# A hybrid encoder layer on one core: the second half's scaled rows are made ahead and kept in DRAM, and TensorE's part of interleaved steps gets a later place in the scheduler's order

## The chip, the cores and the metric

The kernel runs on one NeuronCore of a Trainium2 chip. The metric is the device time of one execution in microseconds (us); before the change it is 1823.78 us, the median of three runs (1821.98 to 1827.82). TensorE (PE in the profile; PEld are its weight loads) multiplies, VectorE (DVE) and ScalarE (ACT) work elementwise, GpSimd (POOL) takes small elementwise work, and SyncE (SP) issues nearly all DMAs from one queue, in order.

## The reference

One encoder layer is applied to two groups of tokens, 1024 (sample) and 256 (prompt), 1280 rows of 2048 features in all, with shared weights. Each group also has 256 memory tokens.

```python
def layer(x, mem, norm_g, w_in, ...):
    hn = rms_norm(x, norm_g)
    proj = hn @ w_in                                   # 2048 -> 4896 columns
    xbc, z_ssd, dt_raw, q, k, v, z_att, mq, z_mem = split_cols(proj, IN_SIZES)
    xbc = silu(centred_dwconv(xbc, conv_w, conv_b))    # 5 taps
    ...                                                # two SSD scans, forward and backward
    o_ssd = rms_norm(y * silu(z_ssd), ssd_norm_g)
    o_att = window_attention(rms_norm(q), rms_norm(k), v, sink) * silu(z_att)
    memn = rms_norm(mem, mem_norm_g)
    mk, mv = split_cols(memn @ w_mem_kv, ...)
    o_mem = softmax(rms_norm(mq) @ rms_norm(mk).T) @ mv * silu(z_mem)
    return x + concat([o_ssd, o_att, o_mem]) @ w_out
```

All inputs are float32.

## The kernel before

**Products in three matmuls.** Every float32 factor of the big products is split into a high part (rounded to the matmul's type, `wh`, `xH`) and a low part (`wl`, `xL`, the rest); a product is high x high + low x high + high x low. A weight tile is loaded into `wraw` (SP, `RB` = 4 buffers), ScalarE writes the high part and VectorE the low part (`wsplit`, lines 200 to 206; `WB` = 3 buffers each). So a *weight block* is one load, one or two pairs of splits, and 12 to 21 matmuls.

**Stages.** The 1280 rows are taken in two halves of 640 (grp 0: sample rows 0 to 639; grp 1: the rest). In order: the products with the memory weights (`mk`, `mv`, 32 blocks of 12 matmuls 128x512), the `q` block of half 0 (16 blocks of 15), the *pair stage* of half 0 (`pairs_in(0)`: 10 units of 8 blocks of 21 matmuls 128x320), the `kv` block (16 of 15, 288 wide) and the `mq` block (16 of 15) of half 0, the pair stage of half 1, and then blocks with *lane steps* beside them, and last the output product.

The pair stage is one level of a Strassen-like scheme with seven products per block (`block_pair`, `seven`): its weights need sums made by GpSimd (`weight_sums`, tile `ws`, split into `sh` and `sl`), and its rows need sums of rows (`p_sums`, split by `p_split` into `tH`, `tL`). At the end of each unit the seven results are added together (`ev_seven`, whose helper tile `yu` has the tag `xst`), and conv or gate work on them is queued in `left`.

**Rows.** Before a half can be multiplied, its rows must be scaled by the norm's gain and by 1/rms of each token (`rbc`, made by `x_rows` with ten small matmuls from `rx`). `rx` needs the sum of squares of each token: `stats` loads pieces of 128x512 and ScalarE squares them with a running sum. `x_stats` does that for half 0; `stage_stats` (before) does it for the remaining five x tiles (20 pieces) and the four tiles of memory tokens (16 pieces), tile `sst`, one buffer with the tag `xst`, called from `pairs_in(0)` at five of the eight blocks of a unit.

For half 1, `t_step` then runs beside the `kv` and `mq` blocks. It loads row tiles from the input (`p_load`), scales them and stores the scaled tile in DRAM (`p_scale`, `xs_d`), makes the sums and splits them, and from step 23 on loads the stored tiles again (`r_load`) and fills `xH`, `xL` of half 1 (`r_fill`, `p_rows`).

**Lanes.** Attention, SSD and memory attention for tiles of 128 tokens are generators in two queues (`lanes`). `pump` takes steps from them after each weight block at fixed rates; `step` runs a generator up to its next `yield`. A step's instructions go to all engines, TensorE's among them, as small matmuls and transposes between those of the weight blocks.

**Order.** The program is not run in the order in which it is written. Every instruction gets a running number; a scheduler fills each engine's queue with what is ready by its own estimate, the lowest number first. `tc.high_priority(offset=n)` gives a lower number by n; a negative offset gives a later one. `tc.issue_after(marks)` queues an instruction behind the last weight split on its own engine. Weight splits and evictions have offsets of 30 to 100 (`HP`). The queues so made are fixed: on the chip each engine works in that order and waits where an operand isn't there.

Of the kernel before, what the change touches and what calls it, by code (L numbers as in the profile page):

```python
# [10 lines left out]
F32 = mybir.dt.float32  # L11
F32R = mybir.dt.float32r
# [13 lines left out]
HP = (30, 100, 100)  # L26
MR = ((1.75, 0), (1.75, 0))
# [14 lines left out]
def hymba_encoder_kernel(  # L42
# [7 lines left out]
    V, A, G, T, S = nc.vector, nc.scalar, nc.gpsimd, nc.tensor, nc.sync  # L50
# [215 lines left out]
    def block_feat(name, evac):  # L266

        ps = [[acc.tile([P, 512], F32, tag="acc", name="acc") for _ in range(2)] for _ in range(2)]
        src = laid_in(name)
        hls = {}  # L270
        for kk in range(KT // 2):
            raw = wp.tile([P, 512], F32, tag="wraw", name="wraw", bufs=RB)
            S.dma_start(raw, src[kk])
            with tc.high_priority(offset=HP[2]):
                h = wp.tile([P, 2, 256], F32R, tag="wh", name="wh", bufs=WB)
                l = wp.tile([P, 2, 256], F32R, tag="wl", name="wl", bufs=WB)
                wsplit(raw, h.rearrange("p a c -> p (a c)"), l.rearrange("p a c -> p (a c)"))
            hls[kk] = h, l
            if kk == KT // 2 - 2:
                continue  # L280
            tail = kk == KT // 2 - 1

            for kks in ([(kk - 1, kk)] if tail else [(kk,)]):
                for f in range(2):
                    for k in [2 * x + j for x in kks for j in range(2)]:
                        q, m = divmod(k, 4)
                        sh, sl = [x[:, k % 2, f * P:(f + 1) * P] for x in hls[k // 2]]
                        for half in range(2):
                            c = slice(half * 320, half * 320 + 320)
                            o = ps[f][half][:, :320]  # L290
                            T.matmul(o, sh, cur["H", q][:, m, c], start=(k == 0), stop=False)
                            T.matmul(o, sh, cur["L", q][:, m, c], start=False, stop=False)
                            T.matmul(o, sl, cur["H", q][:, m, c], start=False, stop=(k == KT - 1))
                    if tail and f == 0:
                        with tc.high_priority(offset=HP[1]):
                            evac(0, ps[0])
            for k in range(2 * kks[0], 2 * kk + 2):
                yield k
        with tc.high_priority(offset=HP[1]):
            evac(1, ps[1])  # L300


    def ev_gate(c, base):
        def f(i, ps):
            z = ev.tile([P, 512], F32, tag="evt" if i % 2 else "evu", name="zs")
            A.activation(z, ps, AF.Tanh, scale=0.5)
            V.scalar_tensor_tensor(out=z, in0=z, scalar=1.0, in1=ps, op0=ALU.add, op1=ALU.mult)
            S.dma_start(z_d[c][base + i], z)
        return f

    def ev_gateT(c, grp, f0):
        def f(fc, ps):
            z = ev.tile([P, 640], F32, tag="evu", name="zs")
            for b in range(2):
                zb, p = z[:, b * 320:b * 320 + 320], ps[b][:, :320]
                A.activation(zb, p, AF.Tanh, scale=0.5)
                V.scalar_tensor_tensor(out=zb, in0=zb, scalar=1.0, in1=p, op0=ALU.add, op1=ALU.mult)
            S.dma_start(zT_d[c][grp][:, f0 + fc, :], z)
        return f
# [24 lines left out]
    def conv_work(grp, fc, u):  # L344
# [5 lines left out]
        def first_tap():  # L350
            c.append(ev.tile([P, 650], F32, tag="evt", name="c")[:, :n])
            A.activation(c[0], u[:, :n], AF.Identity, scale=cw[0], bias=vec[:, R_CB + fc:R_CB + fc + 1])
# [26 lines left out]

    def ev_conv(grp, f0):  # L380
        us = []

        def f(fc, ps):
            fc = f0 + fc
            u = ev.tile([P, 650], F32, tag="evu", name="u")
            V.tensor_copy(u[:, 0:4], carry[:, fc, :])
            V.memset(u[:, 388:392], 0.0)
            V.memset(u[:, 648:650], 0.0)
            A.activation(u[:, 4:324], ps[0][:, :320], AF.Copy)
            A.activation(u[:, 324:388], ps[1][:, :64], AF.Copy)  # L390
            A.activation(u[:, 392:648], ps[1][:, 64:320], AF.Copy)
            us.append(u)
            if len(us) == 2:
                left.extend(conv_two(*[conv_work(grp, f0 + i, us[i]) for i in range(2)]))
        return f
# [85 lines left out]
    def k_prep(t):  # L481
# [3 lines left out]
        ss = sm.tile([P, 2], F32, tag="s2", name="kss", bufs=4)  # L485
# [3 lines left out]
        rr = sm.tile([P, 2], F32, tag="s2", name="krr", bufs=4)  # L489
# [109 lines left out]
    def attn(t):  # L599
# [13 lines left out]
        ss = sm.tile([P, 8], F32, tag="s8", name="qss", bufs=4)  # L613
        V.reduce_sum(out=ss, in_=hv(sq), axis=AX.X)
        r = sm.tile([P, 8], F32, tag="s8", name="qr", bufs=4)
# [27 lines left out]
        def scores(rr):  # L643
            lg = mp.tile([P, 2, 385], F32, tag="lg", name="lg", bufs=2)
            G.tensor_copy(lg[:, :, nk:nk + 1], ns8[:, rr, :].unsqueeze(2))  # L645
            nm = sm.tile([P, 2], F32, tag="m2", name="nm", bufs=10)
# [8 lines left out]
            den = sm.tile([P, 2], F32, tag="m2", name="den", bufs=10)  # L655
# [57 lines left out]
    def mem_attn(t):  # L713
# [26 lines left out]
        def scores(hp):  # L740
# [8 lines left out]
            m = sm.tile([P, 2], F32, tag="m2", name="mm", bufs=10)  # L749
# [3 lines left out]
            den = sm.tile([P, 2], F32, tag="m2", name="mden", bufs=10)  # L753
# [53 lines left out]
    def ssd_up(t):  # L807
# [27 lines left out]
        cbd = sm.tile([P, 2], F32, tag="s2", name="cbd", bufs=4)  # L835
        V.reduce_sum(out=cbd, in_=cd2, axis=AX.X)
        dco = sm.tile([P, 16], F32, tag="dco", name="dco", bufs=2)
# [166 lines left out]
    def ssd_down(t):  # L1004
# [3 lines left out]
        ss = sm.tile([P, 2], F32, tag="s2", name="yss", bufs=4)  # L1008
# [39 lines left out]
        rs = sm.tile([P, 2], F32, tag="s2", name="yrs", bufs=4)  # L1048
# [177 lines left out]
    def p_load(k, grp=0):  # L1226

        raw[k] = [rp.tile([P, 640], F32, tag="ch", name=n, bufs=CH) for n in ("ra", "rb_")]
        for i in range(2):
            r = k + 8 * i  # L1230
            S.dma_start(raw[k][i], x_turned[grp, r * P:(r + 1) * P, :])

    def p_scale(k, grp=0):

        for i, x in enumerate(raw[k]):
            r = k + 8 * i
            V.scalar_tensor_tensor(out=x, in0=x, scalar=vec[:, R_G + r:R_G + r + 1], in1=rbc, op0=ALU.mult, op1=ALU.mult)
            if grp:
                S.dma_start(xs_d[r], x)

    def p_rows(k, tiles):

        for i, x in enumerate(tiles):
            q, j = divmod(k + 8 * i, 4)
            if j == 0:
                new_quad(q)
            h, l = cur["H", q][:, j, :], cur["L", q][:, j, :]
            A.activation(h, x, AF.Copy)
            V.tensor_sub(l, x, h.bitcast(F32))

    def p_fill(k):
        p_scale(k)
        p_rows(k, raw[k])
# [9 lines left out]
    def r_fill(k):  # L1263
        p_rows(k, again.pop(k))
# [14 lines left out]

    p_plan = {}  # L1280
    for k in range(8):
        at = (9, 12, 15, 17, 20, 22, 25, 27)[k]
        sums_at = (at + 1, 32, 34)[max(0, k - 5)]
        for j, f in ((at - 2, p_load), (at, p_fill), (sums_at, p_sums), (sums_at + 1, p_split)):
            p_plan.setdefault(j, []).append((f, k))

    def p_step(j):
        if j == 9:
            need(x_rows, [0])
        with ExitStack() as st:  # L1290
# [4 lines left out]
            for f, k in sorted(p_plan.get(j, ()), key=lambda x: ((p_split, p_sums, p_fill, p_load).index(x[0]), x[1])):  # L1295
# [11 lines left out]
    def t_step(j):  # L1307
        with ExitStack() as st:
# [4 lines left out]
            for f, k in t_plan.get(j, ())[::-1]:  # L1313
                f(k)

    def ev_seven(kind, f0, grp):
# [3 lines left out]
        def begin(u):  # L1320
# [9 lines left out]
            else:  # L1330
                tiles = [ev.tile([P, 650], F32, tag="evu", name="r") for _ in range(2)]
# [210 lines left out]
    squares = stage_stats()  # L1542
# [4 lines left out]
    def pairs_in(grp, extra):  # L1547
# [16 lines left out]
    pairs_in(0, p_step)  # L1564
    for _ in squares:
        pass
    for _ in x_rows(1):
        pass
# [11 lines left out]
    pairs_in(1, t_step)  # L1580
# [183 lines left out]
```

## Time and profile before

| | |
|---|---|
| median of three runs | 1823.78 us (1821.98 to 1827.82) |
| profiled execution, its own time | 1824.83 us |
| its span, first to last instruction | 1823.1 us |
| granted TensorE clock, mean | 0.995 |
| TensorE busy | 1778.3 us, 98% |
| VectorE, ScalarE, GpSimd busy | 1328.4, 950.1, 673.6 us |
| DMA traffic | 329 MB, mean 180 GB/s |

How to read the lines: a group line has the source line, the engine, the operation, out<-in by tile names and the shape, then the count, busy time, mean duration in ns, and the idle time of the engine just before. In the view of waits a row says which engine and tile waited for what: us in total, number of times, longest. In the view of windows each row is a stretch of time with the busy us and number of instructions of each engine, the granted clock, the share of DMA in use and GB/s. In the view of the time line a row is start, duration, engine, line, operation and in brackets the idle time before it and what ended it. A matmul's end is modelled, so short gaps between matmuls don't show as idle time.

### The profile page before, as it was taken

Reading aid. Unit: us, or ns where it says so; the run is one execution under the profiler, and the core shown is the slowest. Engines: PE = TensorE matmul, PEld = TensorE weight load, DVE = VectorE, ACT = ScalarE, POOL = GpSimd, SP = SyncE. Lnnn points to the kernel's source line nnn. Section 1 sums busy time; section 2 is a strip of 40 time slices with the busy share of each in tenths; the row PEclk is TensorE's granted clock in tenths of the full one; section 3 lists DMA queues with packets and bytes.
Section 4 is the critical chain, followed back from the end, with each engine's and each line's share of the span. In section 5 each row is a group of like instructions: output and inputs, shape, how many; then the busy total and the mean of one; then the engine's idle time right before and its main releaser. Section 6 shows DMA issues by size and latency. Waiting matters only on the chain.

```text
span 1823.1 us, 30989 instructions
## 1 busy us (share of the span) xinstructions
PE 1778.3 (98%) x10306; PEld 1572.7 (86%) x10306; DVE 1328.4 (73%) x2473; ACT 950.1 (52%) x2081; POOL 673.6 (37%) x1092
## 2 busy tenths in 40 slices
PE   9999999999999999999999999999999999999999
PEld 7788999999799999987777877887777787889998
DVE  5595678888878889787667767767787765766665
ACT  6554545553454444366567447666547644543332
POOL 0115778870168889411001110001111101048774
PEclk9999999999999999999999999999999999999999
DMA  8685544446853343374545577656688765654442
GB/s 296 196 315 192 152 142 146 128 146 206 265 189 91 114 117 110 106 219 133 162 136 155 165 241 267 207 173 213 220 282 259 238 212 161 201 154 147 142 139 81
DMA packets 213873, 328.96 MB, mean 180 GB/s; under 512 B 21904, under 2 KB 84688, under 8 KB 213712
## 3 DMA queue, kind: packets, MB, share of 16 engines
q1 hardware_dynamic: 213568, 326.92, 57.8%
q8 instruction: 81, 1.33, 0.3%
q14 instruction: 80, 0.66, 0.1%
q10 hardware_dynamic: 144, 0.06, 0.0%
HBM read 250.29 MB, written 76.61 MB: 179 GB/s over the span
## 4 chain that ended last, share of the span: by engine, by line
PE 65%; DMA 12%; issue 8%; DVE 6%; POOL 5%; ACT 3%; SPq 1%; ACTq 0%; POOLq 0%; DVEq 0%
PE acc L257 8%; PE acc L256 8%; PE acc L258 8%; PE acc L1207 7%; PE acc L1205 7%; PE acc L1206 7%; POOL ws L1177 3%; PE accm L1206 3%; PE accm L1205 3%; PE accm L1207 3%; PE py L937 2%; DVE wl L204 1%; DMA wraw<-in_w_in_pairs_dram 1%; DMA rf<-ac 1%; POOL wraw L1177 1%
## 5 line engine op out<-in xcount | busy, mean ns | idle before, releaser
L257 PE MATMUL acc<-wl,xH 128*128 128x512 f32 (+1 forms) x1248 | 479.0, 384 | 8.0 <-DVE wl L204 7.7
L256 PE MATMUL acc<-wh,xH 128*128 128x512 f32 (+1 forms) x1248 | 484.3, 388 | 1.6 <-ACT wh L203 1.5
L258 PE MATMUL acc<-wh,xL 128*128 128x512 f32 (+1 forms) x1248 | 476.0, 382 | 0.0
L204 DVE TENSOR_TENSOR wl<-wraw,wh 128x512 fp32r<-128x512 f32 (+1 forms) x480 | 351.8, 736 | 145.7 <-ACT wh L203 140.5
L203 ACT ACTIVATE wh<-wraw 128x512 fp32r<-128x512 f32 (+1 forms) x480 | 290.8, 612 | 211.1 <-PE acc L258 126.7
L257 PEld LDWEIGHTS acc<-wl,xH 128*128 128x128 f32 x1248 | 236.1, 189 | 54.9 <-DVE wl L204 13.6
L256 PEld LDWEIGHTS acc<-wh,xH 128*128 128x128 f32 x1248 | 236.1, 189 | 45.7 <-ACT wh L203 3.6
L258 PEld LDWEIGHTS acc<-wh,xL 128*128 128x128 f32 x1248 | 235.7, 189 | 42.1 <-issue 0.7
L1177 POOL TENSOR_TENSOR ws<-wraw 128x128 f32<-128x128 f32 x224 | 144.8, 646 | 340.9 <-DMA wraw<-in_w_in_pairs_dram 210.2
L203 ACT ACTIVATE sh<-ws 128x384 fp32r<-128x384 f32 x224 | 115.7, 523 | 272.9 <-PE acc L1206 131.2
L204 DVE TENSOR_TENSOR sl<-ws,sh 128x384 fp32r<-128x384 f32 x224 | 156.2, 700 | 136.9 <-ACT sh L203 132.5
L1177 POOL TENSOR_TENSOR ws<-wraw,ws 128x128 f32<-128x128 f32 x224 | 149.1, 666 | 17.3
L1177 POOL TENSOR_TENSOR ws<-ws,wraw 128x128 f32<-128x128 f32 x224 | 152.8, 682 | 0.0
L1177 POOL TENSOR_TENSOR wraw<-wraw 128x128 f32<-128x128 f32 x224 | 138.9, 620 | 17.5
L645 POOL COPY lg<-nsink 128x2 f32<-128x2 f32 x40 | 17.3, 433 | 268.9 <-PE ppt L673 138.9
L1205 PE MATMUL acc<-xH,wh 128*128 128x320 f32 x320 | 99.5, 311 | 3.7 <-ACT wh L203 3.7
L1207 PE MATMUL acc<-xH,wl 128*128 128x320 f32 x320 | 99.2, 310 | 3.3 <-DVE wl L204 3.3
L1205 PE MATMUL acc<-tH,sh 128*128 128x320 f32 x320 | 99.1, 310 | 1.0 <-ACT qs L324 1.0
L1207 PE MATMUL acc<-tH,sl 128*128 128x320 f32 x320 | 99.2, 310 | 0.0
L1206 PE MATMUL accm<-tL,wh 128*128 128x320 f32 x320 | 99.1, 310 | 0.0
L1205 PE MATMUL accm<-tH,wh 128*128 128x320 f32 x320 | 99.0, 310 | 0.0
L1206 PE MATMUL acc<-xL,wh 128*128 128x320 f32 x320 | 99.0, 309 | 0.0
(479 smaller groups left out, 3921.1 us busy)
## 6 DMA issues: line engine op xcount, KB each, us to landing
wraw<-in_w_in_pairs_dram SPq DMA_DIRECT2D x160, 256.0 KB, 2.8
wraw<-in_w_in_laid_dram SPq DMA_DIRECT2D x128, 256.0 KB, 3.7
wraw<-in_w_out_laid_dram SPq DMA_DIRECT2D x64, 256.0 KB, 3.3
wraw<-in_w_out_pairs_dram SPq DMA_DIRECT2D x64, 256.0 KB, 2.9
xH<-xH SPq DMA_DIRECT2D x16, 640.0 KB, 5.9
xL<-xL SPq DMA_DIRECT2D x16, 640.0 KB, 6.5
rf<-ac SPq DMA_DIRECT2D x40, 256.0 KB, 4.0
rb<-ac SPq DMA_DIRECT2D x40, 256.0 KB, 4.4
```

What stands on the lines that cost most here:

```text
L203: a = A.activation(h, raw, AF.Copy)
L204: b = V.tensor_sub(l, raw, h.bitcast(F32))
L256: T.matmul(ps[t][:, :n], sh, h[:, :n], start=(k_ == 0), stop=False)
L257: T.matmul(ps[t][:, :n], sh, l[:, :n], start=False, stop=False)
L258: T.matmul(ps[t][:, :n], sl, h[:, :n], start=False, stop=(k_ == last))
L645: G.tensor_copy(lg[:, :, nk:nk + 1], ns8[:, rr, :].unsqueeze(2))
L937: T.matmul(py[:, h * 64:h * 64 + 64], mt[:, (h % 4) * P:(h % 4 + 1) * P], xsT[g][:, h * 64:h * 64 + 64], start=True, stop=True)
L1177: G.tensor_tensor(out=o, in0=x, in1=y, op=op)
L1205: T.matmul(ps[p], h, xh, start=(k_ == 0), stop=False)
L1206: T.matmul(ps[p], h, xl, start=False, stop=False)
L1207: T.matmul(ps[p], l, xh, start=False, stop=(k_ == 7))
```

## The change

It has two parts, and some tidying.

First, the scaled rows of half 1 are made during the pair stage of half 0. The generator `first_side` takes the place of `stage_stats` there: it squares the 20 pieces of the five remaining x tiles, runs `x_rows(1)`, and then for each of the 16 row tiles loads it, scales it on VectorE and stores it in `xs_d`. `t_step` loads the scaled tiles (`p_next`) and no longer scales; its steps and those of the second filling move by a few places, and the second filling writes into the row tiles that are there (`new=False`) instead of taking new ones. The 16 pieces of the memory tokens are squared by `next_side`, called in the pair stage of half 1. Both generators use one buffer of their own, tag `sq`.

Second, TensorE's operations go through an object `Later`: those issued inside a lane step, except steps of `x_stats` and `x_rows`, get a number later by `LATE` = 20.

Beside that, unused functions are removed, small tiles move from the pool `sm` to `mp`, and some tiles are cut to the width that they use.

```diff
+LATE = 20
...
-    V, A, G, T, S = nc.vector, nc.scalar, nc.gpsimd, nc.tensor, nc.sync
+    V, A, G, S = nc.vector, nc.scalar, nc.gpsimd, nc.sync
+
+    class Later:
+        inside = False
+
+        def __getattr__(self, op):
+            def issue(*args, **kw):
+                with tc.high_priority(offset=-LATE) if self.inside else ExitStack():
+                    return getattr(nc.tensor, op)(*args, **kw)
+            return issue
+
+    T = Later()
...
                 for ins in marks:
                     st.enter_context(tc.issue_after(ins))
+                T.inside = name[0] not in ("x_stats", "x_rows")
+                st.callback(setattr, T, "inside", False)
                 next(gen)
...
-        ss = sm.tile([P, 2], F32, tag="s2", name="kss", bufs=4)
+        ss = mp.tile([P, 2], F32, tag="s2", name="kss", bufs=4)
...
-    def p_scale(k, grp=0):
-
-        for i, x in enumerate(raw[k]):
-            r = k + 8 * i
-            V.scalar_tensor_tensor(out=x, in0=x, scalar=vec[:, R_G + r:R_G + r + 1], in1=rbc, op0=ALU.mult, op1=ALU.mult)
-            if grp:
-                S.dma_start(xs_d[r], x)
+    def x_row(grp, r):
+        return x_turned[grp, r * P:(r + 1) * P, :]
+
+    def scale_row(r, x):
+        V.scalar_tensor_tensor(out=x, in0=x, scalar=vec[:, R_G + r:R_G + r + 1], in1=rbc, op0=ALU.mult, op1=ALU.mult)
...
-            if j == 0:
+            if new and j == 0:
                 new_quad(q)
...
-        p_rows(k, again.pop(k))
+        p_rows(k, again.pop(k), new=False)
...
+    def p_first(k):
+        p_load(k, lambda r: x_row(0, r))
+
+    def p_next(k):
+        p_load(k, lambda r: xs_d[r])
...
-        at = (3, 6, 9, 12, 15, 17, 19, 21)[k]
-        for j, f in ((at - 2, lambda k: p_load(k, 1)), (at, lambda k: p_scale(k, 1)), (at + 1, p_sums), (at + 2, p_split)):
+        at = (4, 7, 10, 13, 15, 17, 19, 21)[k]
+        for j, f in ((at - 3, p_next), (at, p_sums), (at + 2, p_split)):
             t_plan.setdefault(j, []).append((f, k))
-    for k, at in enumerate((25, 27, 29, 31, 32, 33, 35, 37)):
+    for k, at in enumerate((25, 26, 27, 28, 29, 31, 33, 35)):
         for j, f in ((at - 2, r_load), (at, r_fill)):
...
-    def stage_stats():
-
-        yield from stats([(xrow(t), t) for t in range(5, 10)] + [(mrow(i), 10 + i) for i in range(4)],
-                         lambda i: fin.tile([P, 512], F32, tag="xst", name="sst"), ahead=1, group=3)
+    def square_place(_):
+        return fin.tile([P, 640], F32, tag="sq", name="sst")[:, :512]
+
+    def first_side():
+
+        yield from stats([(xrow(t), t) for t in range(5, 10)], square_place, ahead=1)
+        for _ in x_rows(1):
+            yield
+        for r in range(KT):
+            x = fin.tile([P, 640], F32, tag="sq", name="xrow")
+            S.dma_start(x, x_row(1, r))
+            yield
+            with ExitStack() as st:
+                for ins in marks:
+                    st.enter_context(tc.issue_after(ins))
+                scale_row(r, x)
+                S.dma_start(xs_d[r], x)
+            yield
+
+    def next_side():
+        yield from stats([(mrow(i), 10 + i) for i in range(4)], square_place, ahead=1)
...
-                if k in (0, 2, 4, 5, 7):
-                    next(squares, None)
+                if grp == 0 and (u > 3 or k not in (3, 7)) or grp and k in (0, 2, 4):
+                    next(side, None)
...
-    pairs_in(0, p_step)
-    for _ in squares:
-        pass
-    for _ in x_rows(1):
-        pass
+    side = first_side()
+    pairs_in(0, p_step, side)
+    assert next(side, None) is None
...
-    pairs_in(1, t_step)
+    side = next_side()
+    pairs_in(1, t_step, side)
+    assert next(side, None) is None
```

More of the change, by code (lines that the diff above doesn't have):

```diff
@@ L264, in block_tok @@
             yield k
[L266 to L300, printed above, removed]
     def ev_gate(c, base):
@@ L1007, in ssd_down @@
         tok = slice(t * P, (t + 1) * P)
-        ss = sm.tile([P, 2], F32, tag="s2", name="yss", bufs=4)
+        ss = mp.tile([P, 2], F32, tag="s2", name="yss", bufs=4)
         if not last:
@@ L1047, in ssd_down @@
                 yield
-        rs = sm.tile([P, 2], F32, tag="s2", name="yrs", bufs=4)
+        rs = mp.tile([P, 2], F32, tag="s2", name="yrs", bufs=4)
         rsqrt(rs, ss, 1.0 / 512, 2)
@@ L1330, in begin @@
             else:
-                tiles = [ev.tile([P, 650], F32, tag="evu", name="r") for _ in range(2)]
+                tiles = [ev.tile([P, 640], F32, tag="evu", name="r") for _ in range(2)]
             r0, r1 = [hv(x[:, o:o + 640], 2) for x in tiles]
@@ L1541, in hymba_encoder_kernel, with pairs_in @@
     units = [(i // 2, i % 2 * 2) if i < 4 else (None, 2 * (i - 4)) for i in UNITS]
-    squares = stage_stats()
     owe = 0.0
     keep = [(q, i, j) for q in range(4) for i in range(2) for j in (0, 2)]
-    def pairs_in(grp, extra):
+    def pairs_in(grp, extra, side):
         nonlocal owe
```

60 lines of the change are left out of this document (18 added, 42 removed).

## The prediction

> **What bounds the kernel now.** I read the page's first part, then the windows cut where the kernel's stages change, then TensorE's waits in the stages that lose time, then the rows of the tiles behind those waits.
>
> ```profile
> span 1823.1 us, 30989 instructions
> PE 1778.3 (98%) x10306; PEld 1572.7 (86%) x10306; DVE 1328.4 (73%) x2473; ACT 950.1 (52%) x2081; POOL 673.6 (37%) x1092
> ```
> ```profile
> core 0: us, PE busy (x) PEld busy (x) DVE busy (x) ACT busy (x) POOL busy (x), PEclk, DMA share, GB/s
> 0.00:152.00 152.00, 148.07 (x636) 120.21 (x637) 96.55 (x160) 82.32 (x151) 18.11 (x37) 1.00 0.81 273
> 152.00:413.00 261.00, 252.59 (x1688) 248.44 (x1687) 194.03 (x300) 132.04 (x272) 201.39 (x318) 0.99 0.48 142
> 413.00:445.00 32.00, 30.58 (x233) 30.35 (x232) 25.62 (x47) 11.59 (x23) 3.03 (x4) 1.00 0.60 189
> 445.00:505.00 60.00, 55.61 (x242) 43.79 (x241) 51.78 (x80) 27.36 (x47) 9.29 (x12) 0.98 0.83 267
> 505.00:750.00 245.00, 245.00 (x1652) 243.54 (x1651) 203.93 (x324) 117.24 (x207) 203.93 (x304) 0.99 0.40 120
> 750.00:1560.00 810.00, 787.62 (x4252) 638.71 (x4251) 584.62 (x1293) 477.82 (x1207) 88.40 (x162) 1.00 0.64 199
> ```
> TensorE is the bound: 98% busy, and the change neither adds nor removes a matmul. Only its idle time is at stake. By stage (window minus PE busy): memory projections and the q block 152 - 148.07 = 3.9 us; the first half's pair blocks 261 - 252.59 = 8.4; the kv block 1.4; the mq block 4.4; the second half's pair blocks 0; the blocks with lane steps 810 - 787.62 = 22.4.
>
> The two pair stages do the same matmuls, and the second loses nothing. What differs is the side work, and these rows show how it hurts:
>
> ```profile
> PE acc L1205 <- ACT wh L203: 3.7, 5, 1.2
> PE acc L1207 <- DVE wl L204: 3.3, 7, 0.8
> ```
> ```profile
> L1392 ACT ACTIVATE sst<-sst x36: 613/632/637, 154.7 to 401.3; 128x512 f32<-128x512 f32 x36
> L1392 ACT ACTIVATION_READ_ACCUMULATOR sst<-sst x36: 182/187/189, 155.3 to 401.8; 128x1 f32 x36
> ...
>   ACT sst L1392: 52.4, 29
> ...
> DMA to landing us min/median/max: 2.8/3.3/5.8
> ```
> ```profile
> SPq L1401 <- DVE u L1351: 22.1, 5, 5.8
> SPq L1401 <- ACT sst L1392: 35.4, 23, 3.2
> ```
> ```profile
> 314.99 0.62 ACT L1392 ACTIVATE sst<-sst 128x512 f32<-128x512 f32 x1
> ...
> 319.65 0.63 ACT L1392 ACTIVATE sst<-sst 128x512 f32<-128x512 f32 x1 [0.29 <-DMA sst<-in_mem_sample_dram]
> ...
> 323.71 0.64 ACT L1392 ACTIVATE sst<-sst 128x512 f32<-128x512 f32 x1 [2.11 <-DMA sst<-in_mem_sample_dram]
> ...
> 328.43 0.63 ACT L1392 ACTIVATE sst<-sst 128x512 f32<-128x512 f32 x1 [3.06 <-DMA sst<-in_mem_sample_dram]
> ```
> The 36 squares of the first half's pair stage share one buffer (tag xst), also with the evictions' yu. So each load waits for the square before it (and, at a unit's end, up to 5.8 us for an eviction), each square for its load: a chain of 3.3 landing + 0.63 + 0.19 = 4.1 us, and the three distances above, 4.66, 4.06 and 4.72, agree; I take 4.2. ScalarE does its work in order, so the splits wh and sh behind a waiting square are late, and after a group of four TensorE stops at the next unit: 3.7 + 3.3 = 7.0 us.
>
> **What goes.** (a) The changed kernel gives the squares a buffer of their own (tag sq). In its built order no square stands between the 9th and the 76th of the 80 weight blocks of that stage. So the 7.0 us at unit starts go, and with them a stretch at half clock that followed one of them:
>
> ```profile
> 253.20:256.60 3.40, 3.40 (x15) 0.50 0.51 152
> 502.40:509.20 6.80, 6.08 (x14) 0.50 0.95 327
> ```
> At full clock the second pair stage starts a matmul every 245 / 1652 = 0.148 us, so 3.4 us would hold 23, not 15: 8 x 0.148 = 1.2 us. Together -8.2.
>
> The Trainium skill (TensorE: Matmul & The Clock Gate, section HAM oscillation) warns of gaps over some 3.4 us. This trace is stricter: the single idle times before both stretches are all under 1.5 us, and the clock was halved nevertheless.
>
> (b) The second half's 16 scalings and 16 stores leave the row filling in the kv and mq blocks:
>
> ```profile
> PE acc L257 <- DVE wl L204: 4.2, 6, 1.4
> PE acc L256 <- ACT wh L203: 1.5, 2, 1.1
> ```
> ```profile
> L1237 DVE SCALAR_TENSOR_TENSOR ra<-ra,vec,rbc x16: 876/879/1082, 76.7 to 481.8; 128x640 f32<-128x640 f32 x16
> ```
> TensorE loses 4.2 + 1.5 = 5.7 us there. The half-clock stretch costs more: 14 matmuls in 6.8 us, where at the 0.237 us of the first window (148.07 us, with 624 block matmuls and a dozen small ones) 29 fit: 15 x 0.237 = 3.6 us. VectorE sheds 16 x 0.88 = 14 us. But the worst cluster, just before 502, stands at the second filling of the x rows, which stays and is even put on consecutive steps (25 to 29). I count half of 9.3 us: -4.6, bounds 0 and -9.3.
>
> (c) Lane matmuls get a number 20 later. What they lose now:
>
> ```profile
> PE pst L867 <- DVE fl L888: 3.1, 2, 2.0
> ...
> PE psc L651 <- ACT qT L635: 0.3, 1, 0.3
> ```
> These are the first and last of 15 kinds of lane wait that, with one of a weight split, make up the 22.4 us of the last window. Their cause is the scheduler's guess: a lane matmul is put where its operand should be ready, and the operand comes 0.3 to 2 us later. A later number helps only where priority, not readiness, set the place. In the built order lane matmuls do move back, by 5 to 8 of the 15 matmuls of a weight block in the mean. But their feeding operations move back too: of 500 lane matmuls that wait for something, those with under 2 us of matmuls between the last matmul that their operand depends on and themselves fall from 135 to 100, while the median distance doesn't change and some get shorter (probability transposes pmt among them). A quarter fewer tight places would be 0.26 x 22.4 = -6; new tight ones could give +4. I take -2.
>
> **What comes.** Durations of the two kinds of chain:
>
> ```profile
> xst<-in_x_sample_dram SPq DMA_DIRECT2D x20, 256.0 KB, 4.3
> ...
> ra<-in_x_turned_dram SPq DMA_DIRECT2D x16, 320.0 KB, 3.8
> zT<-th SPq DMA_DIRECT2D x16, 320.0 KB, 2.8
> ```
> ```profile
> L204 DVE TENSOR_TENSOR wl<-wraw,wh 128x512 fp32r<-128x512 f32 (+1 forms) x480 | 351.8, 736 | 145.7 <-ACT wh L203 140.5
> L203 ACT ACTIVATE wh<-wraw 128x512 fp32r<-128x512 f32 (+1 forms) x480 | 290.8, 612 | 211.1 <-PE acc L258 126.7
> ```
> The cover is the splits' lead: three buffers, so a split may run while two blocks of matmuls remain, in the pair stage 2 x 21 x 0.148 = 6.2 us less 0.61 + 0.74 and the sums' splits, some 4 us.
>
> (d) Eight of the 20 squares of the other x rows are pulled ahead into the memory projections' end: in the built order the first stands after weight block 23 and the eighth after block 33. One buffer, and DMAs at a share of 0.81: 4.3 + 0.63 + 0.19 = 5.1 us each, so 7 x 5.1 = 35.7 us, against nine blocks of 12 and one of 15 matmuls, 123 x 0.237 = 29.2. The surplus is 6.5. There the lead is nearly used up by the 20 squares before them, so I take +5 (0 to +6.5). The other 12 stand 5 us apart in the q block and the first units, further than their chain.
>
> (e) The 16 squares of the memory tokens, planned for the second pair stage, are pulled before it: nothing holds their ScalarE part back, and the scheduler sees ScalarE free. In the built order 14 stand between weight block 76 of the first pair stage and block 15 of the kv block: 13 x 4.2 = 54.6 us, against 4 x 21 x 0.148 + 15 x 2.0 (32 us for 16 kv blocks) = 42.4. Surplus 12.2, less the lead of 4 to 6: +7 (0 to +12). SP's weight loads queue behind these loads too, each held until the square before it is done.
>
> (f) The 16 rows scaled ahead share that one buffer: store, then load, then scaling, 2.8 to 3.6 + 3.8 + 0.88, some 7.8 us with the nearest rows, 7.6 with the lighter traffic here. VectorE waits for the load, and the splits wl and sl stand behind it; SP waits for the store with weight loads behind it. The built order spreads the 16 scalings over 34 blocks, 34 x 3.11 = 105.7 us; 15 x 7.6 = 114. Surplus 8, less the lead: +4 (0 to +9). VectorE's 14 us of extra work themselves are free: the second pair stage runs it at 203.93 / 245 = 83% without loss, and here it would be at (194 + 14) / 261 = 80%.
>
> By the Trainium skill (DMA: Bandwidth & Descriptors, section on the anatomy of one DMA: 2.0 us fixed and the bytes at 436 GB/s) a 320 KB transfer would take an estimated 2.75 us, a row 6.4 us, and (f) would be nothing; the rows above, 2.8 and 3.8, don't agree for loads.
>
> (g) Stalls of several us in (d) and (e) bring half-clock stretches: 1.2 us for one as in (a), 3.6 for a double one: +3.
>
> The tile renames, the moved small tiles, the removed unused functions and 16 more loads (5 MB, at a DMA share near 0.5) cost nothing.
>
> Sum: -8.2 - 4.6 - 2 + 5 + 7 + 4 + 3 = +4.2. The profiled execution took 1824.83 us, so 1829.0. That is 1 us above the median of 1823.78, a difference I don't correct for.
>
> **The rivals.** *Faster: the chains are hidden.* The lead recovers between squares, and chains at their shortest landing of 2.8 leave only +3 of (d) to (g); then -8.2 - 4.6 - 6 + 3 = -16: 1809; with (b) at its best -9.3, 1804; with the lanes at -2, 1813. For it: squares with a buffer of their own start their load earlier than now. Against it: 29 of the 36 sst squares waited for their load. Chance 0.28, decided by landing plus square staying within some 3.7 us: 13 x 3.7 = 48 leaves (e) inside the lead. The price of the Trainium skill's page above lies on this side, for the rows alone.
>
> *Slower: the square chain owns the kv block.* The row chain (f) has eaten the lead just before the first memory-token square comes; then the surpluses aren't covered: 6.5 + 12.2 + 8 + 3 against 8.2 + 4.6 + 2: +15, 1840. It decides from a lead under 1 us at block 75. For it: rows and squares follow each other in the same buffer. Chance 0.32.
>
> *Nothing gained in lanes and the filling, (b) and (c) zero or worse:* +11, 1836; its chance is in the one before.
>
> *The change does not do what it says:* the later number moves no matmul. The built order excludes it.
>
> **How the numbers follow.** This kernel can be told from no change at about 0.3%, 5.5 us. My forecast, the partial trade of stalls, has 0.40; its own range is 1822 to 1836, so of it 0.27 lies within 0.3% and 0.13 slower. The faster case gives 0.27 faster and 0.01 same, the slower one 0.28 slower and 0.04 same. So faster 0.27, same 0.32, slower 0.41. Range 1811 to 1842: it reaches from the hidden chains to the bare ones.
>
> **What would show it.** Right: no idle time of TensorE at unit starts before 260 us; sst squares around 400 to 440 us 4 us apart, each with a DMA wait; kv blocks longer than 2.0 us; VectorE waiting for DMA xrow; lane waits near 20 us. Wrong: the window of the kv block still loses under 2 us (then e fails), VectorE's waits for xrow under 5 us in all (f fails), or lane waits under 12 us (c was underrated).

## The result, and the profile after

The changed kernel takes 1841.64 us (median of four runs, 1840.2 to 1844.44), the kernel before beside it 1823.5: a ratio of 1.0097, with a 95% interval of 1.0077 to 1.0118. It is slower by 18 us. (One run of the kernel before, of 2147 us at a granted clock of 0.753, is left out of all comparisons.) The forecast was 1829.0; the result lies at the upper edge of the range (1811 to 1842) and 1.6 us from the rival "slower: the square chain owns the kv block" (1840).

The first part of the page after the change:

```profile
span 1842.7 us, 31031 instructions
PE 1795.1 (97%) x10306; PEld 1579.8 (86%) x10306; DVE 1329.8 (72%) x2473; ACT 951.6 (52%) x2081; POOL 671.4 (36%) x1092
```

TensorE's matmuls are the same in number, but it is busy 16.8 us longer and idle 2.8 us longer. More busy time for the same matmuls means here that the clock was halved for a time or that matmuls followed each other at a slower pace; both are seen below. To see where, both profiles are cut where each stage issues its first block matmul. The columns are those of the windows in the prediction. First the kernel before:

```profile
0.00:154.00 154.00, 150.07 (x644) 121.89 (x645) 96.55 (x160) 82.42 (x151) 19.71 (x40) 1.00 0.81 274
154.00:414.40 260.40, 251.99 (x1691) 248.16 (x1690) 195.43 (x303) 132.81 (x272) 199.79 (x314) 0.99 0.48 140
414.40:447.80 33.40, 31.98 (x244) 31.75 (x242) 27.02 (x49) 13.05 (x26) 3.03 (x4) 1.00 0.62 192
447.80:512.00 64.20, 59.81 (x243) 46.54 (x242) 50.67 (x77) 27.80 (x47) 13.43 (x20) 0.95 0.84 275
512.00:757.50 245.50, 245.50 (x1682) 245.49 (x1681) 206.51 (x332) 115.77 (x205) 199.78 (x296) 1.00 0.38 114
757.50:1621.40 863.90, 841.51 (x4470) 681.70 (x4469) 623.06 (x1354) 503.15 (x1249) 97.84 (x178) 1.00 0.64 198
```

The changed kernel, at the same six stages:

```profile
0.00:166.70 166.70, 156.88 (x645) 124.25 (x645) 97.54 (x163) 90.83 (x182) 21.68 (x46) 0.97 0.81 267
166.70:426.60 259.90, 252.53 (x1691) 248.75 (x1690) 210.56 (x311) 117.65 (x219) 203.32 (x302) 0.99 0.51 160
426.60:469.10 42.50, 36.88 (x243) 35.07 (x242) 28.66 (x57) 21.71 (x50) 3.87 (x8) 0.92 0.68 206
469.10:525.40 56.30, 55.00 (x243) 44.95 (x241) 41.28 (x70) 29.93 (x51) 14.22 (x22) 1.00 0.80 255
525.40:772.20 246.80, 246.22 (x1682) 245.95 (x1681) 199.99 (x320) 112.77 (x199) 195.39 (x296) 1.00 0.36 108
772.20:1641.90 869.70, 850.42 (x4470) 683.91 (x4470) 622.09 (x1354) 503.51 (x1249) 92.79 (x178) 0.99 0.64 197
```

Half clock comes in stretches of 3.4 us or 6.8 us in these two profiles. Such a stretch is counted here with half its length: a stage's length times (1 - granted clock). "At full clock" below means that this is taken off.

| stage | before | after | difference | of it half clock |
|---|---|---|---|---|
| memory projections and q block | 154.0 | 166.7 | +12.7 | +5.1 |
| first pair stage | 260.4 | 259.9 | -0.5 | 0 |
| kv block | 33.4 | 42.5 | +9.1 | +3.4 |
| mq block | 64.2 | 56.3 | -7.9 | -3.4 |
| second pair stage | 245.5 | 246.8 | +1.3 | 0 |
| blocks with lane steps | 863.9 | 869.7 | +5.8 | +3.4 |
| output product | 201.7 | 200.8 | -0.9 | 0 |

The sum is +19.6, the difference of the spans. (The profiled execution after, 1844.44 us, is the longest of the four, so it is more than the 18 us of the medians.) In the kv block the time line of ScalarE shows the forecast chain of squares (start, duration, and in brackets the idle time before and what ended it):

```profile
426.52 0.63 ACT L1346 ACTIVATE sst<-sst 128x512 f32<-128x512 f32 x1 [2.78 <-DMA sst<-in_mem_sample_dram]
...
430.63 0.63 ACT L1346 ACTIVATE sst<-sst 128x512 f32<-128x512 f32 x1 [3.39 <-DMA sst<-in_mem_sample_dram]
...
431.26 1.09 ACT L217 ACTIVATE wh<-wraw 128x288 fp32r<-128x288 f32 x3
434.90 0.63 ACT L1346 ACTIVATE sst<-sst 128x512 f32<-128x512 f32 x1 [2.56 <-DMA sst<-in_mem_sample_dram]
```

The squares start 4.1 and 4.3 us apart, each after waiting for its load, and the weight splits are done in a bunch between them. TensorE's waits in this stage:

```profile
PE acc L59 <- ACT wh L217: 4.2, 2, 3.0
PE acc L59 <- DVE wl L218: 1.0, 2, 0.6
```

In the changed kernel all of TensorE's operations carry line 59, the line of `Later`; the tile names tell them apart.

### The profile page after: what moved, and what is told of

Same layout as the page of the kernel before. It is cut to its first block, busy times and chain, and to the rows that moved or that the text cites. A ratio compares the mean times of both kernels' runs of the same rounds, so it can differ in the third digit from the quotient of the medians.

```text
span 1842.7 us, 31031 instructions
## 1 busy us (share of the span) xinstructions
PE 1795.1 (97%) x10306; PEld 1579.8 (86%) x10306; DVE 1329.8 (72%) x2473; ACT 951.6 (52%) x2081; POOL 671.4 (36%) x1092
## 5 line engine op out<-in xcount | busy, mean ns | idle before, releaser
L59 PE MATMUL acc<-wh,xH 128*128 128x512 f32 (+1 forms) x1248 | 490.8, 394 | 10.3 <-ACT wh L217 8.6
L59 PE MATMUL acc<-wl,xH 128*128 128x512 f32 (+1 forms) x1248 | 489.7, 392 | 8.9 <-DVE wl L218 8.2
L59 PE MATMUL acc<-wh,xL 128*128 128x512 f32 (+1 forms) x1248 | 487.9, 391 | 0.0
L59 PEld LDWEIGHTS acc<-wh,xH 128*128 128x128 f32 x1248 | 237.9, 191 | 59.6 <-ACT wh L217 11.9
L1127 POOL TENSOR_TENSOR ws<-wraw 128x128 f32<-128x128 f32 x224 | 146.5, 654 | 259.4 <-DMA wraw<-in_w_in_pairs_dram 93.0
L1127 POOL TENSOR_TENSOR ws<-wraw,ws 128x128 f32<-128x128 f32 x224 | 153.8, 687 | 17.6
L1127 POOL TENSOR_TENSOR ws<-ws,wraw 128x128 f32<-128x128 f32 x224 | 148.4, 663 | 0.0
L595 POOL COPY lg<-nsink 128x2 f32<-128x2 f32 x40 | 12.5, 314 | 285.7 <-PE ppt L59 118.5
L59 PE MATMUL acc<-tL,sh 128*128 128x320 f32 x320 | 98.7, 308 | 0.0
```

Source lines behind the costliest of these rows:

```text
L59: return getattr(nc.tensor, op)(*args, **kw)
L1127: G.tensor_tensor(out=o, in0=x, in1=y, op=op)
```

## The experiments

**The later number alone, and the rows alone.** The first kernel is the one before with `Later` and `LATE = 20`; the second is the changed one without them:

```diff
-    T = Later()
+    T = nc.tensor
...
-                T.inside = name[0] not in ("x_stats", "x_rows")
-                st.callback(setattr, T, "inside", False)
```

> The kernel before with one part of the change: lane matmuls numbered 20 later; rows and squares as before. In its built order TensorE passes from weight blocks to lane matmuls 465 times (222 before, 466 in the changed kernel). Theory S (the later number costs by itself: the alternation adds small losses at each passage, more than the distances won give back): the stages up to 757 us stay as before, the lane stage takes 869 to 872 us instead of 863.9, the time is 1829 to 1833 us. Rival R (readiness, step (c) of the prediction: the shift is neutral or gains, and the lane stage's +5.8 us in the changed kernel came from the moved small tiles, the cut buffers or another starting point): lane stage 858 to 865, time 1817 to 1825.

> The changed kernel without the later number: the rows scaled ahead, the squares' own buffer and all tidying stay. Theory S with the stage sums of the two traces (+2.9 +9.7 -0.5 +9.0 -7.9 +1.3 -0.9, and 0 in the lane stage): 1835 to 1838 us, lane stage 864 +- 2, kv stage 42, memory and q stages 12 us over before. Rival R: the lane stage keeps its +5.8 and the time is that of the changed kernel, 1841.

Measured: the later number alone 1828.3 us, ratio 1.002 (1.0004 to 1.0036), so some 3.7 us, between the ranges of theory S (from 1829) and rival R (to 1825); the rows alone 1842.34, ratio 1.0095 (1.0068 to 1.0121), some 17 us, near rival R's 1841 and above theory S's 1838. Nearly all of the loss comes with the rows and squares. The later number costs 3 to 4 us by itself, not -2; on top of the rows nothing more of it can be seen (1841.64 against 1842.34), within the scatter. The blocks with lane steps, before and with the later number alone:

```profile
757.50:1621.40 863.90, 841.51 (x4470) 681.70 (x4469) 623.06 (x1354) 503.15 (x1249) 97.84 (x178) 1.00 0.64 198
```
```profile
754.80:1622.10 867.30, 847.72 (x4470) 680.88 (x4470) 622.42 (x1354) 502.76 (x1249) 93.92 (x178) 1.00 0.63 197
```

TensorE's idle time falls from 22.4 to 19.6 us: the distance to the operands did help, by about what was forecast. But its busy time rises by 6.2 us for the same 4470 matmuls, with 3.4 us of half clock in both. With the rows alone the stage is 869.5 us long too, though the order of its matmuls is that of before. So the stage's length decides nothing: over the seven kernels here with that order it takes 858.6 to 864.9 us at full clock, and 862.9 to 865.3 in the three whose lane matmuls all have the later number.

Its two parts do decide. Busy time less half clock is 837.4 to 838.3 us in the seven and 843.6 to 844.3 us in the three; idle time is 24.0 us in the mean (20.6 to 26.8) and 20.0 (19.3 to 21.2). The later number saves some 4 us of waiting and adds some 6 us of busy time.

**The squares held.** `stats` gets a list of instructions behind which the square is queued on ScalarE; first for the memory tokens only, then for the x rows also:

```diff
-                    A.activation(x, x, AF.Square, accum_out=s4[:, c:c + 1])
+                    with ExitStack() as st:
+                        for ins in held:
+                            st.enter_context(tc.issue_after(ins))
+                        A.activation(x, x, AF.Square, accum_out=s4[:, c:c + 1])
...
-        yield from stats([(mrow(i), 10 + i) for i in range(4)], square_place, ahead=1)
+        yield from stats([(mrow(i), 10 + i) for i in range(4)], square_place, ahead=1, held=marks)
```

> As the kernel with the rows alone, and the 16 squares of the memory tokens are queued behind the last weight split on ScalarE, so that none stands ahead of the second pair stage (in the built order the first is at weight block 158 of 224 instead of 124; the pair stage begins at 144). Theory Q (step (e): the square chain owns the kv block): the kv stage falls from 42 to 33 or 34 us, its half-clock stretch goes, the second pair stage loses 0 to 3, the time is 6 to 9 us under the kernel with the rows alone, 1827 to 1831. Rival K (the kv block is held by the row chain or by weight loads behind the scaled rows' stores): the kv stage stays over 39 us and the time within 2 us of the kernel with the rows alone.

> As the kernel before this one, and the 20 squares of the other x rows held too (the first at weight block 38, the second at 47, the rest up to 80, instead of 23 to 57). Theory Q: the memory and q stages, 161.3 us in the changed kernel, fall back to the 148.7 of before, and the first pair stage, whose units then begin with squares again at 3 to 6 us from each other, loses 0 to 6: time 6 to 12 us under the one with only the memory squares held, 1817 to 1824. Rival M (the stalls of the squares only move): the first pair stage loses what the q stage gains, 10 us or more, and the time stays within 3 us of the one with only the memory squares held.

Measured: 1830.23 us, ratio 1.0035 (1.0019 to 1.005), with the memory squares held; 1826.26, ratio 1.0002 (0.9987 to 1.0018), with all held. The kv block with the rows alone, and with the memory squares held:

```profile
425.20:468.00 42.80, 36.63 (x241) 34.84 (x240) 28.61 (x57) 21.34 (x50) 3.88 (x8) 0.92 0.67 203
```
```profile
424.90:456.50 31.60, 31.60 (x242) 31.60 (x241) 25.50 (x50) 13.88 (x28) 2.58 (x4) 1.00 0.57 180
```

All idle time of the kv block and its half clock are gone: 11.2 us, of it 7.8 at full clock. So the squares own that block, not the weight loads behind the row stores (rival K). Holding the x squares takes the memory projections and the q block back at full clock, from the first block matmul on, to 149.4 us; the four kernels that pull them ahead have 156.1 to 156.6, the kernel before 148.6. That is 7 us, and the first pair stage loses only 1.2 of them (258.2 to 259.4). The time falls by 4.0 us, 2 us short of what theory Q expected, but rival M, that the stalls only move, falls too.

**The rows left out, and the rows in two buffers.** In the first of these kernels the 16 rows are not made ahead at all, and half 1 is computed from unscaled rows. In the second, whose squares are all held, each row takes another buffer than the one before it:

```diff
-            x = fin.tile([P, 640], F32, tag="sq", name="xrow")
+            x = fin.tile([P, 640], F32, tag=("sq", "xst")[r % 2], name="xrow")
```

> As the kernel with the memory squares held, but the 16 rows of half 1 are neither loaded, scaled nor stored in the first pair stage; the later loads take the unscaled rows from the input, in the same number and size, so half 1 is computed from unscaled rows. Theory F (the row chain is what fills the place of the lost unit-start stalls): the first pair stage falls from 259.9 us (258.2 at full clock) to 250 to 253, the rest is the same, the time 5 to 9 us under the kernel with the memory squares held (1830.2). Rival U (the first pair stage loses what it loses by its own work, sums, evictions and conv work; the rows are free): the stage stays at 257 or more, the time within 3 us.

> As the kernel with all squares held, and the 16 rows take the buffers sq and xst in turn, so that a row's load needn't wait for the store of the row before it. Theory F (a chain of store, load and scaling in one buffer): VectorE's waits for xrow fall from 8.5 us to under 3, the first pair stage from 262.8 us (259.4 at full clock) to 253 to 257, the time from 1826.3 to 1820 to 1823, below the kernel before. Rival G (the other user of xst, the evictions' yu at a unit's end, now waits for a row to be stored): stage at 259 or more, stalls at unit starts, time 1825 to 1832.

Without the rows: 1824.44 us, ratio 0.9977 (0.9952 to 1.0001). The first pair stage with the memory squares held, with and without rows:

```profile
165.00:424.90 259.90, 252.32 (x1691) 248.73 (x1690) 210.66 (x311) 114.73 (x209) 201.53 (x300) 0.99 0.50 156
```
```profile
165.20:415.20 250.00, 247.82 (x1691) 246.97 (x1690) 195.44 (x295) 115.28 (x210) 193.87 (x300) 1.00 0.40 122
```

The stage is 9.9 us shorter, 8.2 at full clock. That is theory F: the row chain costs 8.2 us, and it hides that the unit-start stalls are gone. With two buffers for the rows the time is 1823.43 us, ratio 0.9983 (0.9965 to 1.0001), and the stage takes 253.7 us at full clock instead of 259.4. VectorE's waits for a row's load, a row in the kernel with one buffer, don't occur any more in the view of the other:

```profile
DVE xrow L1174 <- DMA xrow<-in_x_turned_dram: 8.5, 8, 2.2
```

So of the 8.2 us some 5.7 are the one buffer; what the other 2.5 are is not shown. The intervals of the two kernels' run times overlap (0.9987 to 1.0018 with one buffer), so here the stage carries the argument.

**The later number with all squares held.** The changed kernel with the squares held as above; it differs from the earlier one by the later number alone.

> The changed kernel, later number included, with all squares held; it differs from the kernel with all squares held by the later number alone. Theory S (later number costs by itself, as it did alone on the kernel before, 1.002): 1828 to 1831 us, lane stage 3 to 4 us longer at full clock than the 859.7 of that kernel, with less idle time of TensorE in it. Rival N (what it cost there was scatter; the changed kernel and the one without the later number were equal at 1841.6 and 1842.3): 1824 to 1827.

Measured: 1830.24 us, ratio 1.0018 (1.0003 to 1.0034), against 1.0002 without the later number. The lane stage has 844.0 us of busy time less half clock instead of 837.4, and 21.2 us of idle time instead of 22.3. This is what theory S expected again, by the ratios some 3 us, though the two intervals overlap.

**The price of a passage.** Only matmuls, of three kinds, in groups or one by one:

```diff
+            for i in range(160 // g):          # g = 8, then g = 1
+                for j in range(g):
+                    block(big, ...)            # 128x128 weights, 512 columns
+                for j in range(g):
+                    f(small, j)                # one of the three small kinds
```

> The price of a passage by itself; only TensorE's matmuls are in it, on fixed data, and the layer isn't computed. After a warm-up, three kinds of small matmul (128x128 float32 transpose as ppt, 128x128 transpose in the block's own type as pq, 128x64 by 256 float32 as po) are run with 160 block matmuls of 128x512 each, once in groups of 8 and 8 (20 passages), once one by one (160 passages), all operands in place. Theory S: the one-by-one stretch is longer by 20 to 60 ns for each of the 140 more passages, 3 to 8 us a kind. Rival Z (a passage costs nothing when the operand is there; the later number costs through late operands): under 1 us a kind.

The windows of the six stretches, in the order float32 transpose grouped and one by one, transpose in the block's type, 64-wide float32 product:

```profile
76.50:129.20 52.70, 52.70 (x314) 45.29 (x313) 0.00 (x0) 0.00 (x0) 0.00 (x0) 1.00 0.00 1
129.70:184.00 54.30, 54.26 (x318) 43.15 (x317) 0.12 (x1) 0.00 (x0) 0.00 (x0) 1.00 0.00 1
186.50:235.80 49.30, 49.30 (x315) 41.86 (x313) 0.00 (x0) 0.00 (x0) 0.00 (x0) 1.00 0.00 1
236.40:291.00 54.60, 54.55 (x318) 43.07 (x316) 0.07 (x1) 0.00 (x0) 0.00 (x0) 1.00 0.00 1
293.70:404.70 111.00, 111.00 (x474) 69.31 (x473) 0.00 (x0) 0.00 (x0) 0.00 (x0) 1.00 0.00 1
405.50:564.00 158.50, 158.50 (x478) 59.93 (x477) 0.53 (x1) 0.00 (x0) 0.00 (x0) 1.00 0.00 0
```

For 140 more passages, each into the small kind and back: 1.6 us, 5.3 us and 47.5 us. The windows of the second of each pair hold 3 or 4 matmuls more, which is part of the first two differences. The distance from one passage to the next is free of that: in the time line it is 2.716, 2.550 and 5.647 us for eight and eight in the mean, and 0.344, 0.346 and 1.006 us for one and one. That makes 5, 31 and 342 ns for each passage more. TensorE is 100% busy in all six, so such a cost never shows as idle time or as a wait. The first kind is under what theory S expected, the second inside it, the last far over it. This is one execution, and it does not say whether the width, the type or the shape of the last kind makes its price.

**The later number, but not for po.**

```diff
-                    T.matmul(hv(po[kv * 64:kv * 64 + 64, :2 * P], 2), v_all[...], ...)
+                    nc.tensor.matmul(hv(po[kv * 64:kv * 64 + 64, :2 * P], 2), v_all[...], ...)
```

> As the kernel with the later number alone, but the 64-wide products of step values (tile po) keep their number. Passages into po fall from 26 to 12 (14 in the kernel before), runs of po from 29 to 22 (20 before), all passages only from 465 to 442. By the measured price (about 0.34 us for a passage into and out of po, 0.01 to 0.04 for the transposes) theory S expects 9 fewer runs of po x 0.34 = 3 us less in the lane stage: 1824 to 1827, close to the kernel before. Rival L (the later number costs through its other passages, or through operands that come late): 1828 to 1830 as before this edit.

Measured: 1820.47 us beside 1822.8 for the kernel before, ratio 0.9999 (0.9984 to 1.0015); with po later it was 1.002. The lane stage:

```profile
755.50:1617.30 861.80, 843.27 (x4470) 682.14 (x4470) 621.88 (x1354) 502.93 (x1249) 92.72 (x178) 1.00 0.63 198
```

Idle 18.5 us, and busy time is down by 4.5 us to 843.3 with the same half clock, though 442 of the 465 passages are still there. So the place of po makes most of the 6 us of busy time. The price of a passage fits that roughly: runs of po fall from 29 to 22 (by 7, not by the 9 of the expectation), 2.4 us at 342 ns, and passages from blocks into po from 26 to 12, 4.8 us. That it is the passage, and not something else about po's place, is argued from this and not shown. The two intervals of the run times overlap, so the size (3 to 4 us) is not sharp. The microseconds lie under both expectations because the kernel before, too, is faster beside this run (1822.8 against 1825.3).

**Squares and rows in two buffers.** The squares, too, take `sq` and `xst` in turn.

> As the kernel whose rows alternate between sq and xst, and the squares alternate too. Theory F (one buffer makes the chain, for squares as for rows): a square's load no longer waits for the square before it, the first pair stage falls by another 1 to 3 us from 253.7 at full clock, the time is 1819 to 1822. Rival G (squares that hold xst make the evictions at unit ends late again, the kernel before's 7.0 us of step (a)): stalls on wh or wl at unit starts in the first half of the stage, stage at 256 or more, time 1824 to 1830.

Measured: 1817.57 us beside 1822.8, ratio 0.9981 (0.9965 to 0.9996). This is the one version here whose whole interval lies under the kernel before, by 0.2%. Theory F's further gain in the first pair stage did not show (256.9 us at full clock in this profile, 253.7 in the other, TensorE still waiting 3.8 us for wl and once 3.1 us for ws). That length is rival G's mark, but its sign is missing: these waits stand at 270 us and later, not at unit starts of the stage's first half, and the time is under both expectations. The memory projections and the q block are at 147.4, the kv block at 31.6.

## Why the prediction was wrong in size, step by step

The forecast's outcome, a partial trade of stalls, named the right places but came out 12.6 us low. The rival that it gave 0.32 has the right time, but not for its reason (below).

- **(a) right.** -8.2 forecast; without the rows the first pair stage takes 250.0 us against 258.7 at full clock before, -8.7. (The 1.2 us of half clock in the forecast did not go: the changed kernel has a stretch of 3.4 us in this stage too, at 395.9 us.) In the changed kernel TensorE's only wait between 160 and 300 us is one of 1.4 us (prx for ws).
- **(b) direction right, size between the value taken and the bound.** -4.6 forecast. In the six kernels with the memory squares held, all without scalings there, the kv and mq blocks take 88.1 to 91.2 us together, against 97.6 before: 6.4 to 9.5 less, of it 3.4 the half-clock stretch, which doesn't return. The worst cluster before 502 us was thought to stay; it went with the rest.
- **(c) wrong sign.** -2 forecast, about +3 measured (+2 by busy and idle time, +3 to +4 by two pairs of kernels, none to be seen by the third), inside its bounds (-6 to +4). The readiness reasoning held: idle time fell by some 4 us, and the forecast "lane waits near 20 us" came true (869.7 - 850.42 = 19.3). The failing step was to price lane matmuls by their waits alone. The built order had 222 passages from blocks to lane matmuls before and 466 after (in the lane stage the traces show 220 and 463), and busy time rose by 6 us, most of it with the place of po.
- **(d) too small, and in another place.** +5 forecast; 7.6 us at full clock and 5.1 us of half clock in the profile. The eight squares beside the memory projections cost less than forecast: the q block begins at 100.2 us instead of 97.3. The other 4.6 us at full clock lie in the q block, where the forecast had nothing. The step that failed is "The other 12 stand 5 us apart in the q block and the first units, further than their chain." At the end of the q block the squares still waited for their loads, and splits and TensorE behind them. Two of these squares, and TensorE's waits from 100 to 167 us:

```profile
159.50 0.63 ACT L1346 ACTIVATE sst<-sst 128x512 f32<-128x512 f32 x1 [4.38 <-DMA sst<-in_x_prompt_dram]
...
164.16 0.63 ACT L1346 ACTIVATE sst<-sst 128x512 f32<-128x512 f32 x1 [2.94 <-DMA sst<-in_x_prompt_dram]
```
```profile
PE acc L59 <- DVE wl L218: 2.5, 2, 1.4
PE acc L59 <- ACT wh L217: 1.9, 1, 1.9
PE acc L59 <- ACT mvo L372: 1.6, 1, 1.6
```

- **(e) right.** +7 forecast, 7.8 at full clock: the surplus of 12.2 less a lead of 4.4. Squares 4 us apart and kv blocks of 42.5 / 16 = 2.7 us came as forecast.
- **(f) half of what it was.** +4 forecast (0 to 9), 8.2 measured. The chain was right: by the view of the tile xrow the 16 scalings run from 282.0 to 399.4 us, 117.4 / 15 = 7.8 us apart. Two sizes failed. With 7.8 us for 7.6 the surplus is 117.4 - 105.7 = 11.7 us, not 8; and less of it was covered by the lead: TensorE paid 8.2 us at full clock and a half-clock stretch (1.7 us) at 395.9, which leaves some 2 us for the lead, not 4. That view, the page's DMA issues and SP's waits show what the chain is made of:

```profile
L1186 DVE SCALAR_TENSOR_TENSOR xrow<-xrow,vec,rbc x16: 867/1004/1112, 282.0 to 399.4; 128x640 f32<-128x640 f32 x16
```
```profile
xrow<-in_x_turned_dram SPq DMA_DIRECT2D x16, 320.0 KB, 3.2
...
xs<-xrow SPq DMA_DIRECT2D x16, 320.0 KB, 2.2
```
```profile
SPq L1378 <- DVE xrow L1186: 28.0, 16, 3.7
```

  A load and a store of 3.2 and 2.2 us and a scaling of 1.0 make 6.4 us. SP stands before each store for 1.75 us on average (28.0 / 16) until the scaling is done, and the scaling has its place behind weight splits on VectorE. So part of the distance is TensorE's own pace, and the chain's share in it can't be told apart further.

  The Trainium skill (DMA: Bandwidth & Descriptors, section on the anatomy of one DMA) had given an estimated 6.4 us a row from its 2.0 us and 436 GB/s, a fit for transfers that GpSimd issues; these are SP's. The trace agrees with that sum, but not with its parts: the estimate is 2.75 us for either transfer, and the load took 3.2 and the store 2.2. And yet the rows stood 7.8 us apart.

- **(g) too small in this profile, too large over the runs.** Half clock cost 17.1 us in the profile after and 8.5 in the one before. Over all runs the median loss, span times (1 - granted clock), is 10.0 us for the kernel before, 11.0 with the rows alone, 10.1 and 11.9 with squares held, and 10.1 in the changed kernel's own four runs: 0 to +2, not +3.

At full clock the measured terms are -8.7 - 4.4 (the six kernels' mean, 89.8, against 94.2) + 3 + 7.6 + 7.8 + 8.2 = +13.5; up to two us of half clock come on top. The remaining 3 to 4 of the 18 us are within the scatter of such sums and not explained further.

The rival's time came true, but its condition, a lead under 1 us at block 75, was not met. TensorE stood idle for 2.9 us at 391 us, still in the row chain, with the lead used up. This stop gave the lead back: ScalarE then stood 4.1 us until TensorE had read a buffer that it wanted to fill.

```profile
394.63 0.42 PE L59 MATMUL acc<-xH,wl 128*128 128x320 f32 x1 [2.94 <-DVE wl L218]
```
```profile
399.60 0.96 ACT L217 ACTIVATE sh<-ws 128x384 fp32r<-128x384 f32 x2 [4.08 <-PE acc L59]
...
404.90 0.63 ACT L217 ACTIVATE wh<-wraw 128x512 fp32r<-128x512 f32 x1 [0.32 <-PE accm L59]
```
```profile
406.66 0.68 DVE L218 TENSOR_TENSOR wl<-wraw,wh 128x512 fp32r<-128x512 f32 x1
```
```profile
410.95 0.31 PE L59 MATMUL acc<-xH,wh 128*128 128x320 f32 x1
411.09 0.31 PE L59 MATMUL acc<-xL,wh 128*128 128x320 f32 x1
411.24 0.31 PE L59 MATMUL acc<-xH,wl 128*128 128x320 f32 x1
```

The splits of the 76th of the stage's 80 weight blocks end at 405.5 and 407.3 us, and TensorE first reads them at 410.9 and 411.2: a lead of 5.4 and 3.9 us. TensorE's next stop, 3.0 us on a split behind a square, comes only at 428 us, in the kv block, when five of the memory squares had been done before that block. So (e) as it was forecast, with the lead taken off, is the right account, and the rival hit 1840 by luck: its (e) of 12.2 was 4.4 too large, and its (c) of -2 was 5 too small.

## What to carry to other kernels

A side chain (load, small operation, store) in one buffer runs at its own pace, and the in-order engines that carry it make the main work wait. Compare its length with the work beside it, and give it a second buffer or tie it to its place before adding work to it. A stop of TensorE gives the splits their lead back, as at 391 us here, so the next chain does not start from nothing. When small matmuls are moved between large ones, count the passages between the two kinds and what kind they are, not only the operands' waits: the price sits in TensorE's busy time, and that time, less half clock, repeats far better from kernel to kernel (within 1 us of 838 here) than the length of the stage (within 6).

## What the runs showed of the hardware that was not expected

A passage between a 128-wide block matmul and a 64-wide float32 product and back costs some 340 ns, one to a transpose 5 or 31 ns, all of it inside busy time.

In a kernel where TensorE is 98% busy, half-clock stretches cost about 10 us in the median run, and they go with more than half of the scatter: over 28 runs of the kernel before, the granted clock went from 0.991 to 0.997, a loss of 16 to 5 us, and it and the span go together (correlation -0.74). So stages of two profiles are best compared with these stretches taken off.

The Trainium skill (TensorE: Matmul & The Clock Gate, section HAM oscillation) speaks of gaps over 3.4 us. The trace does not agree: the changed kernel's stretch at 105.8 us follows a single idle time of 1.6 us.
